# Dilation-4 score products with stationary operands from tiles ordered by residue of 4, and value tiles of 65 columns

## The chip, the cores and the metric

One core of a Trainium2 chip runs the whole program. The metric is the device time of one execution, in microseconds (us); the lower the better. The kernel before was timed three times: 3049.63, 3056.54 and 3057.88 us, median 3056.54 us.

## The reference

One layer of an encoder over 2048 positions in float32: RMSNorm, a combined projection, eight heads of dilated attention, four mLSTM heads, an output projection, a convolutional GLU feed-forward block, a gated per-layer embedding, and a final norm. The change touches the attention alone. Of it this much matters:

```
ATTN_HEADS = 8; ATTN_HEAD_DIM = 64; SEQ = 2048
ATTN_PATTERNS = ((128, 1), (512, 4), (2048, 16))      # (window, dilation)

def dilated_branch(q, k, v, dil, n_side):
    M = S // dil
    def to_res(t):                                     # residue classes of the positions
        return t.reshape(B, H, M, dil, hd).transpose(0, 1, 3, 2, 4)
    o, lse = banded_attention(to_res(q), to_res(k), to_res(v), n_side)
    ...

def dilated_mixture_attention(q, k, v, positions):
    ...
    for window, dil in ATTN_PATTERNS:
        o, l = dilated_branch(q, k, v, dil, (window // 2) // dil)
        outs.append(o); lses.append(l)
    wts = jax.nn.softmax(jnp.stack(lses, axis=0), axis=0)
    out = jnp.sum(wts[..., None] * jnp.stack(outs, axis=0), axis=0)
```

Each head sees every query against 64 keys on either side in three patterns: neighbours (dilation 1), every fourth position (dilation 4) and every sixteenth (dilation 16). The three are joined by their softmax denominators, so one set of exponentials against one row maximum per query, summed over the three patterns, gives the same result.

## The kernel before

All of it is in the class Attention (L823 to L1137). A head's scores are computed in 16 units of 128 rows for each pattern, called p = 0 (dilation 1), p = 1 (dilation 4) and p = 2 (dilation 16). They are computed twice.

**pass_a** gets the row maxima. Its stationary operand is queries (128 of them), its moving operand a window of keys; each unit takes two matmuls (L949 and L950, a main part and a low part of 65 rows), DVE adds a mask and takes the maximum (L958). It goes in 20 steps: p = 0 in 8 steps of two units, p = 1 in 8 of two, p = 2 in 4 of four. Then come transposes (L962) and a small exchange through DRAM that leaves the negated maxima in a row of qm2.

**pass_b** makes the output, with keys stationary and queries moving (L991, L992 in `weights`). ACT takes the exponential (L996), POOL clears what lies outside the band (L930, L932), and three steps later (LOOK = 3) `values` multiplies by the value tile vt, whose last 64 columns are ones, so that the same product gives the denominators (L1017 for p = 2, L1037 for the others). ACT copies the p = 2 result to oacc (L1018), DVE adds the others (L1047). The steps are p = 2 first (4 steps), then p = 1 (8 steps, called s1 to s8 here), then p = 0 (8 steps).

**The two passes overlap.** `run` takes one step of the stream (pass_a of the next head, and what hangs on it) beside each step of pass_b: step n of pass_b of head h stands beside step 9 + n of pass_a of head h + 1, and after twelve steps beside the first steps of head h + 2. In steady state one head takes one period. At a period's start stand `outputs` of the head just finished: denominators from DRAM and back (zc, zr_d, zb), and two products of 64x1024 on DVE that make att (L1080).

**Layouts.** qs, ks1 and ks2 are loaded in the order of positions (L863 to L865). For dilation 16, km1, km2, qm1 and qm2 hold them ordered by residue of 16. They are made by casts whose source has a stride of 64 bytes: ACT makes km1 (L875), DVE makes km2 and qm1 (L877), four pieces of 512 columns each. For dilation 4 there is no such tile: `unit` returns as stationary operand a slice of qs, ks1 or ks2 with a stride of four elements,

```
t0 = r + 512 * j
return (lambda t: t[:, t0:t0 + 509:4]), ...
```

**Pages.** The large tiles (qs, ks1, ks2, km1, km2, qm1, qm2, vt, oacc, att) take pages from one pool of 22 of 2080 floats per partition. A tile that is asked for when none is free waits until an older one has had its last reader. The pairs of e and the tiles zb share another pool of four. Every engine works through its own queue in order; the order in each queue is set when the kernel is built, by a scheduler that sees dependences and free pages.

Of the kernel before, what the change touches and what calls it, by code (L numbers as in the profile page):

```python
# [828 lines left out]
class Attention:  # L829


    def __init__(self, g, pool, psA):
# [10 lines left out]

        def load_v(h, p):
            if h == 0:
                vt.append(page(g, [P, 16, P], F32, name="vt"))
                nc.gpsimd.memset(vt[p][:, :, HD:], 1.0)
            src, dst = g.vd[h], vt[p][:, :, :HD]
            if p == 0:
                nc.sync.dma_start(dst, src.rearrange("(j p) c -> p j c", p=P))  # L850
            elif p == 1:
                for r in range(4):
                    nc.sync.dma_start(dst[:, 4 * r:4 * r + 4], src.rearrange("(j p r) c -> r p j c", p=P, r=4)[r])
            else:
                nc.sync.dma_start(dst, src.rearrange("(p r) c -> p r c", r=16))

        def load(h):
            H = Head()
            H.qs = page(g, [P, S], F32R, name="qs")
            H.ks1 = page(g, [P, S], F32R, name="ks1")  # L860
            H.ks2 = page(g, [65, S], F32R, name="ks2")
            for s in range(2):
                nc.sync.dma_start(H.qs[64 * s:64 * s + 64].bitcast(F32), g.qk[0, s, h])  # L863
                nc.sync.dma_start(H.ks1[64 * s:64 * s + 64].bitcast(F32), g.qk[1, 0, h])
            nc.sync.dma_start(H.ks2.bitcast(F32), g.kl[h])  # L865
            return H
# [12 lines left out]
        def keys_by_residue(H, q):  # L879
# [4 lines left out]
            to_residues(nc.scalar, H.km1, H.ks1, q)  # L884
            to_residues(nc.vector, H.km2[:64], H.ks2[:64], q)

        def queries_by_residue(H, q):
            if q == 0:
                H.qm1 = page(g, [P, S], F32R, name="qm1")
                H.qm2 = page(g, [65, S], F32R, name="qm2")  # L890
            to_residues(nc.vector, H.qm1, H.qs, q)
            if q == 3:
                nc.sync.dma_start(H.qm2[:64].bitcast(F32), H.qm1[:64].bitcast(F32))

        def unit(p, i):


            if p == 0:
                lo, hi = max(0, 8 * i - 4), min(P, 8 * i + 12)
                return (lambda t: t[:, P * i:P * i + P]), (lambda t: residues(t)[:, :, lo:hi]), lo, hi, lo - (8 * i - 4)  # L900
            if p == 1:
                r, j = divmod(i, 4)
                lo, hi = max(0, 32 * j - 16), min(P, 32 * j + 48)
                t0 = r + 512 * j
                return (lambda t: t[:, t0:t0 + 509:4]), (lambda t: t.rearrange("p (b r a) -> p r b a", r=4, a=P)[:, r, :, lo:hi]), lo, hi, lo - (32 * j - 16)
            return (lambda t: t[:, P * i:P * i + P]), (lambda t: t[:, P * i:P * i + P]), 0, P, 0

        def width(p, lo, hi):
# [28 lines left out]
        def pass_a(h, H):  # L937

            mst = pool.tile([P, 3, 16], F32, name="mst", tag="mst", bufs=2)
            for p in (0, 1, 2):  # L940
                per = 4 if p == 2 else 2
                W = 512 // per
                for i0 in range(0, 16, per):
                    ps = psA.tile([P, 512], F32, name="psa", tag="psa")
                    for u in range(per):
                        st, win, lo, hi, off = unit(p, i0 + u)
                        o = shape3(p, ps[:, u * W:u * W + width(p, lo, hi)], lo, hi)
                        q = st(H.qm1 if p == 2 else H.qs)
                        nc.tensor.matmul(o, lhsT=q, rhs=win(H.km1), start=True, stop=False)  # L949
                        nc.tensor.matmul(o, lhsT=q[:65], rhs=win(H.km2), start=False, stop=True)  # L950
                    for u in range(per):
# [26 lines left out]
        def weights(h, H, p, i0):  # L978
# [9 lines left out]
            for u in range(per):  # L988
                st, win, lo, hi, off = us[u]
                o = shape3(p, ps[:, u * W:u * W + widths[u]], lo, hi)  # L990
                nc.tensor.matmul(o, lhsT=st(H.km1 if p == 2 else H.ks1), rhs=win(H.qm1), start=True, stop=False)  # L991
                nc.tensor.matmul(o, lhsT=st(H.km2 if p == 2 else H.ks2), rhs=win(H.qm2), start=False, stop=True)  # L992
            for u0, u1 in ([(0, per)] if min(widths) == W else [(u, u + 1) for u in range(per)]):
                cs = slice(u0 * W, (u1 - 1) * W + widths[u0])
                st, win, lo, hi, off = us[u0]
# [13 lines left out]
        def values(h, H, p, i0, ew):  # L1009
# [2 lines left out]
            W = 128 if p == 2 else 256  # L1012
            if p == 2:
                b = i0 // 4
                o = self.psO.tile([P, 512], F32, name="pso", tag="pso")
                for u in range(4):
                    nc.tensor.matmul(o[:, P * u:P * u + P], lhsT=vt[2][:, i0 + u, :], rhs=e[:, P * u:P * u + P], start=True, stop=True)  # L1017
                nc.scalar.activation(oacc[:, 512 * b:512 * b + 512], o, AF.Copy)  # L1018
# [3 lines left out]
            for u in range(2):  # L1022
# [7 lines left out]
                for b, x0, x1 in pieces:  # L1030
                    first = b not in banks
                    if first:
                        banks[b] = self.psO.tile([P, 512], F32, name="pso", tag="pso")
                    base = 0 if p == 1 else 32 * b
                    o = banks[b].rearrange("p (x y) -> p x y", y=A)[:, :, x0 - base:x1 - base]
                    m = shape3(p, e[:, cs], lo, hi)[:, :, x0 - lo:x1 - lo]
# [10 lines left out]
                    nc.vector.tensor_tensor(o, o, banks.pop(b).rearrange("p (x y) -> p x y", y=A), ALU.add)  # L1047

        def pass_b(h, H):
            H.oacc = page(g, [P, S], F32, name="oacc")  # L1050
            H.banks = {}
            steps = [(2, i) for i in range(0, 16, 4)] + [(p, i) for p in (1, 0) for i in range(0, 16, 2)]
            pend = []
            for k, (p, i0) in enumerate(steps):
                pend.append((p, i0, weights(h, H, p, i0)))
                if p == 2 and i0 == 12:
                    H.km1 = H.km2 = None
                if len(pend) > LOOK:
                    values(h, H, *pend.pop(0))
                yield  # L1060
# [25 lines left out]
        def stream():  # L1086
            for q in range(4):
                keys_by_residue(heads[0], q)
            for h in range(AH):
                H = heads[h]  # L1090
                n = 0
                for _ in pass_a(h, H):
                    n += 1
                    if n == 10 and h + 1 < AH:
                        heads[h + 1] = load(h + 1)
                    if n in (7, 9, 11, 13):
                        queries_by_residue(H, (n - 7) // 2)
                    if n in (14, 16, 18, 20) and h + 1 < AH:
                        keys_by_residue(heads[h + 1], (n - 14) // 2)
                    yield  # L1100
                H.qs = None

        def start():
            heads[0] = load(0)
# [1242 lines left out]
```

## Time and profile before

| what | value |
|---|---|
| time, median of three | 3056.54 us |
| the profiled execution's time | 3060.42 us |
| its span | 3058.6 us |
| PE busy in the span | 94% |
| DVE, ACT, POOL busy | 66%, 42%, 35% |
| mean granted clock of PE | 0.958 |
| one head's period in the attention | 49.5 us |

The span is one execution from its first instruction to its last; 1.8 us lie around it. The attention's steady state runs from about 720 us to some 1010 us of the span. PE is the engine of matmuls and PEld its loading of stationary operands, which overlaps it; a granted clock of 1.0 is 2.4 GHz and 0.5 is 1.2 GHz. Each load of a stationary operand belongs to one matmul; the distance between the starts of two loads in a row is what one product takes on PE when nothing else holds it.

### The profile page before, as it was taken

The numbers are of one execution on the slowest core, as the hardware profiler recorded it, in microseconds if no ns is written. First come the engines' busy times: TensorE is split into PE (matmuls) and PEld (weight loads), VectorE is DVE, ScalarE is ACT, GpSimd is POOL, SyncE is SP. The second block draws the span as 40 slices with busy tenths as digits, with TensorE's granted clock in tenths as the row PEclk, the third lists the DMA queues.
The fourth block names the chain that finished last, engine by engine and source line by source line (L and its number), as shares of the span: only waits on it lengthen the run. The fifth ranks groups of instructions, "written<-read, shape, count | busy, mean of one in ns | idle before, by whom it ended". The sixth has DMA issues, their size and how long they took to land.

```text
span 3058.6 us, 41026 instructions
## 1 busy us (share of the span) xinstructions
PE 2875.3 (94%) x14474; PEld 2437.7 (80%) x14474; DVE 2032.9 (66%) x4107; ACT 1278.4 (42%) x2428; POOL 1084.5 (35%) x1146
## 2 busy tenths in 40 slices
PE   8889899889999898898899998899999999999999
PEld 7867888789999787786688886688887777877887
DVE  5856796666665488335877777977776566746444
ACT  5555465424333356223544444444444322224332
POOL 2133423416555454001433333433334230433221
PEclk9999999879999999999899999899999999999999
DMA  7744425475554374565222223222225876765111
GB/s 213 213 138 131 140 84 178 130 150 120 121 118 108 107 252 132 141 201 186 69 83 83 79 75 119 66 78 80 83 83 167 315 251 216 245 222 182 44 44 44
DMA packets 386798, 419.77 MB, mean 137 GB/s; under 512 B 107457, under 2 KB 300865, under 8 KB 380945
## 3 DMA queue, kind: packets, MB, share of 16 engines
q1 hardware_dynamic: 386592, 417.16, 44.9%
q8 instruction: 114, 1.87, 0.3%
q14 instruction: 92, 0.75, 0.1%
HBM read 308.16 MB, written 104.61 MB: 135 GB/s over the span
## 4 chain that ended last, share of the span: by engine, by line
PE 46%; DVE 7%; DMA 5%; issue 3%; POOL 3%; ACT 1%; SPq 1%; POOLq 0%; DVEq 0%; ACTq 0%
PE ps L1811 8%; PE ps L1812 8%; PE ps L1813 8%; PE ps L149 6%; PE ps L147 6%; PE ps L148 6%; DMA ar<-a_d 2%; POOL ar L175 1%; DVE fw L176 1%; DVE as L176 1%; DMA wdr<-in_w_ffn_down_dram 1%; PE psm L1480 1%; PE psm L1481 1%; PE psm L1389 1%; DVE bl L176 1%
## 5 line engine op out<-in xcount | busy, mean ns | idle before, releaser
L1811 PE MATMUL ps<-bh,fw 128*128 128x512 f32 x1232 | 495.7, 403 | 28.9 <-ACT fw L176 11.4
L1813 PE MATMUL ps<-bh,fw 128*128 128x512 f32 x1232 | 491.3, 399 | 6.8 <-DVE fw L176 6.7
L1812 PE MATMUL ps<-bl,fw 128*128 128x512 f32 x1232 | 492.9, 400 | 4.1 <-DVE bl L176 3.2
L175 POOL TENSOR_TENSOR sum<-fraw 128x512 f32<-128x512 f32 x132 | 197.7, 1498 | 406.6 <-DVE fw L176 360.2
L1811 PEld LDWEIGHTS ps<-bh,fw 128*128 128x128 f32 x1232 | 236.1, 192 | 94.0 <-ACT fw L176 13.7
L1813 PEld LDWEIGHTS ps<-bh,fw 128*128 128x128 f32 x1232 | 236.2, 192 | 64.6 <-DVE fw L176 10.0
L1812 PEld LDWEIGHTS ps<-bl,fw 128*128 128x128 f32 x1232 | 236.1, 192 | 60.9 <-DVE bl L176 7.4
L147 PE MATMUL ps<-wd,as 128*128 128x512 f32 x616 | 246.1, 399 | 13.8 <-ACT as L176 13.8
L149 PE MATMUL ps<-wd,as 128*128 128x512 f32 x616 | 246.1, 400 | 6.6 <-DVE as L176 6.5
L175 POOL TENSOR_TENSOR ar<-ar 128x768 f32<-128x768 f32 x80 | 141.1, 1785 | 298.7 <-DMA ar<-a_d 220.3
L148 PE MATMUL ps<-wd,as 128*128 128x512 f32 x616 | 244.7, 397 | 0.0
L176 ACT ACTIVATE fw<-sum 128x512 fp32r<-128x512 f32 x220 | 134.6, 628 | 241.7 <-DVE sum L175 142.7
L176 DVE TENSOR_TENSOR fw<-sum,fw 128x512 fp32r<-128x512 f32 x220 | 214.2, 988 | 7.9 <-ACT fw L176 7.7
L176 ACT ACTIVATE as<-ar 128x768 fp32r<-128x768 f32 x108 | 85.0, 792 | 273.6 <-POOL ar L175 222.6
L996 ACT ACTIVATE e<-psb 128x512 f32<-128x512 f32 (+2 forms) x240 | 95.7, 437 | 218.4 <-PE psb L992 205.8
L176 DVE TENSOR_TENSOR as<-ar,as 128x768 fp32r<-128x768 f32 x108 | 111.1, 1037 | 110.1 <-ACT as L176 109.9
L930 POOL TENSOR_SCALAR_AFFINE_SELECT e<-e 128x64 f32<-128x64 f32 (+2 forms) x225 | 102.3, 455 | 202.0 <-ACT e L996 197.6
L1884 POOL TENSOR_TENSOR act<-act,up 128x512 f32<-128x512 f32 x88 | 129.4, 1470 | 87.8 <-DVE up L1833 68.8
L958 DVE CUSTOM_DVE_ANT_0 junk<-psa,mask 128x256 bf16<-128x256 f32 (+1 forms) x304 | 111.7, 367 | 71.9 <-PE psa L950 62.4
L147 PEld LDWEIGHTS ps<-wd,as 128*128 128x128 f32 x616 | 117.4, 191 | 42.9 <-ACT as L176 16.9
L149 PEld LDWEIGHTS ps<-wd,as 128*128 128x128 f32 x616 | 117.3, 190 | 38.8 <-DVE as L176 12.1
L1875 DVE SCALAR_TENSOR_TENSOR act<-ext,fcw,act 128x512 f32<-128x512 f32 (+1 forms) x176 | 136.4, 815 | 16.7 <-ACT act L1873 16.0
(359 smaller groups left out, 7735.9 us busy)
## 6 DMA issues: line engine op xcount, KB each, us to landing
ar<-a_d SPq DMA_DIRECT2D x94, 384.0 KB
ar<-a_d SPq DMA_DIRECT2D x94, 320.0 KB
wdr<-in_w_ffn_down_dram SPq DMA_DIRECT2D x50, 512.0 KB
fraw<-in_w_ffn_gate_dram SPq DMA_DIRECT2D x22, 1024.0 KB
fraw<-in_w_ffn_up_dram SPq DMA_DIRECT2D x22, 1024.0 KB
a_d<-act SPq DMA_DIRECT2D x88, 256.0 KB
xT_d<-xT SPq DMA_DIRECT2D x32, 512.0 KB
bx<-xT_d SPq DMA_DIRECT2D x16, 1024.0 KB
```

Of the source, the lines that this page charges most:

```text
L147: g.nc.tensor.matmul(out, lhsT=sh, rhs=mh, start=start, stop=False)
L148: g.nc.tensor.matmul(out, lhsT=sh, rhs=ml, start=False, stop=False)
L149: g.nc.tensor.matmul(out, lhsT=sl, rhs=mh, start=False, stop=stop)
L175: eng[0].tensor_tensor(src, a, b, ALU.add if sign > 0 else ALU.subtract)
L176: return (lambda: g.nc.scalar.activation(hi, src, AF.Copy)), (lambda: eng[1].tensor_tensor(lo, src, hi.bitcast(F32), ALU.subtract))
L930: nc.gpsimd.affine_select(l, l, pat + [[s, half - off]], ALU.is_ge, 0.0, base=s * off + w, channel_multiplier=-1)
L958: nc.vector.tensor_tensor_reduce(shape3(p, junk[:, :n], lo, hi), o, m, 1.0, -3e38, ALU.add, ALU.max, mst[:, p, i:i + 1])
L1811: nc.tensor.matmul(ps, lhsT=w[:, 0, k], rhs=h[:, k], start=start and k == 0, stop=False, skip_group_check=True)
L1812: nc.tensor.matmul(ps, lhsT=w[:, 0, k], rhs=l[:, k], start=False, stop=False, skip_group_check=True)
L1813: nc.tensor.matmul(ps, lhsT=w[:, 1, k], rhs=h[:, k], start=False, stop=k == 3, skip_group_check=True)
L1875: nc.vector.scalar_tensor_tensor(act, ext[a][:, lo + k:hi + k], self.cw[:, k, f:f + 1], act, ALU.mult, ALU.add)
L1884: nc.gpsimd.tensor_tensor(act, act, up[a][:, lo:hi], ALU.mult)
```

## The change

New tiles hold the queries and keys ordered by residue of 4: q4, k41 and k42. Each is made from qs, ks1 or ks2 by four ACT copies of 512 columns (`to_four`), whose source has a stride of 16 bytes and whose destination is contiguous: twelve copies a head, 96 in all. The p = 1 products of both passes take contiguous slices of them as stationary operand; the moving operands stay as they are. The copies of q4 stand at steps 2, 4, 6 and 8 of the stream, those of k41 and k42 at steps 17 to 20. qs is released at step 13 rather than at the pass's end.

The value tile shrinks from 128 to 65 columns (one column of ones), its three tiles take two pages rather than three, and oacc and its PSUM tiles have 65 partitions in use.

```
-                vt.append(page(g, [P, 16, P], F32, name="vt"))
-                nc.gpsimd.memset(vt[p][:, :, HD:], 1.0)
+                if p != 1:
+                    vt.append(page(g, [P, 2 - p // 2, 16, HD + 1], F32, name="vt"))
+                    nc.gpsimd.memset(vt[p][:, :, :, HD:], 1.0)
+                    vt[p:] = [vt[p][:, i] for i in range(2 - p // 2)]
...
+        def by_four(t):
+            return t.rearrange("p (r m) -> p r m", r=4)
+
+        def to_four(dst, src, r):
+            nc.scalar.activation(by_four(dst)[:, r], src.bitcast(F32).rearrange("p (m r) -> p r m", r=4)[:, r], AF.Copy)
+
+        def queries_by_four(H, r):
+            if r == 0:
+                H.q4 = page(g, [P, S], F32R, name="q4")
+            to_four(H.q4, H.qs, r)
+
+        def keys_by_four(H, r):
+            if r == 0:
+                H.k41 = page(g, [P, S], F32R, name="k41")
+                H.k42 = page(g, [65, S], F32R, name="k42")
+            to_four(H.k41, H.ks1, r)
+            to_four(H.k42, H.ks2, r)
...
-                t0 = r + 512 * j
-                return (lambda t: t[:, t0:t0 + 509:4]), ...
+                return (lambda t: t[:, P * i:P * i + P]), ...
...
-                        q = st(H.qm1 if p == 2 else H.qs)
+                        q = st((H.qs, H.q4, H.qm1)[p])
...
-                nc.tensor.matmul(o, lhsT=st(H.km1 if p == 2 else H.ks1), rhs=win(H.qm1), start=True, stop=False)
-                nc.tensor.matmul(o, lhsT=st(H.km2 if p == 2 else H.ks2), rhs=win(H.qm2), start=False, stop=True)
+                nc.tensor.matmul(o, lhsT=st((H.ks1, H.k41, H.km1)[p]), rhs=win(H.qm1), start=True, stop=False)
+                nc.tensor.matmul(o, lhsT=st((H.ks2, H.k42, H.km2)[p]), rhs=win(H.qm2), start=False, stop=True)
...
-                o = self.psO.tile([P, 512], F32, name="pso", tag="pso")
+                o = self.psO.tile([P, 512], F32, name="pso", tag="pso")[:HD + 1]
...
-            H.oacc = page(g, [P, S], F32, name="oacc")
+            H.oacc = page(g, [HD + 1, S], F32, name="oacc")
...
+                if p == 1 and i0 == 14:
+                    H.k41 = H.k42 = None
...
+                    if n in (2, 4, 6, 8):
+                        queries_by_four(H, (n - 2) // 2)
                     if n in (7, 9, 11, 13):
                         queries_by_residue(H, (n - 7) // 2)
+                    if n == 13:
+                        H.qs = None
+                    if n == 16:
+                        H.q4 = None
+                    if 17 <= n < 21:
+                        keys_by_four(H, n - 17)
                     if n in (14, 16, 18, 20) and h + 1 < AH:
                         keys_by_residue(heads[h + 1], (n - 14) // 2)
                     yield
-                H.qs = None
```

Since the queues are ordered by a scheduler, the new copies and the changed demand for pages move other instructions. Three places of one period in the middle of the attention show it.

ACT, from step s3 of p = 1 on, before. Each p = 1 step has one exponential 192 wide and one 256 wide.

```order
L996 ACTIVATE e<-psb 128x192
L996 ACTIVATE e<-psb 128x256
L1018 ACTIVATE oacc<-pso 128x512
L996 ACTIVATE e<-psb 128x256
L996 ACTIVATE e<-psb 128x192 x2
L996 ACTIVATE e<-psb 128x256 x2
L996 ACTIVATE e<-psb 128x192 x2
L996 ACTIVATE e<-psb 128x256 x2
L996 ACTIVATE e<-psb 128x192 x2
L996 ACTIVATE e<-psb 128x256
```

The same stretch after; L895 is the copy of `to_four`, with k for k41 (9247) and k42 (9248) and q for q4.

```order
L895 ACTIVATE k_9247<-ks_8453 128x512
L1017 ACTIVATE e<-psb 128x256
L1017 ACTIVATE e<-psb 128x192
L895 ACTIVATE k_9247<-ks_8453 128x512 x3
L1017 ACTIVATE e<-psb 128x192
L1017 ACTIVATE e<-psb 128x256 x2
L1017 ACTIVATE e<-psb 128x192 x2
L1017 ACTIVATE e<-psb 128x256
L895 ACTIVATE k_9248<-ks_8454 65x512 x4
L895 ACTIVATE q_9435<-qs 128x512
L1017 ACTIVATE e<-psb 128x256
L1017 ACTIVATE e<-psb 128x192
```

The twelve copies stand between exponentials that followed each other before: one after s3, three after s4, five after s7, three more after s8.

DVE, around the two products att of `outputs`, before. mask1 is the mask of p = 1, mask2 that of p = 2.

```order
L958 ISA junk_7330,mst_7033<-psa_7323,mask1_5786 128x256
L958 ISA mst_7033 128x1
L877 CAST km2_7362<-ks2_7249 64x512
L1080 TENSOR_TENSOR att_7392<-oacc_6663,zb_7279 64x8x128
L877 CAST km2_7362<-ks2_7249 64x512
L958 ISA junk_7357,mst_7033<-psa_7352,mask1_5786 128x256
L958 ISA mst_7033 128x1
L1080 TENSOR_TENSOR att_7392<-oacc_6663,zb_7281 64x8x128
```

And after, where the maxima of p = 2 are already in front of it.

```order
L979 ISA junk_7520,mst_7061<-psa_7509,mask2_5794 128x128
L979 ISA mst_7061 128x1
L979 ISA junk_7522,mst_7061<-psa_7509,mask2_5794 128x128
L979 ISA mst_7061 128x1
L1103 TENSOR_TENSOR att_7425<-oacc_6681,zb_7312 64x8x128
L979 ISA junk_7524,mst_7061<-psa_7509,mask2_5794 128x128
L979 ISA mst_7061 128x1
L1103 TENSOR_TENSOR att_7425<-oacc_6681,zb_7314 64x8x128
```

The first att stood behind one or two of the four casts of km2 and the early p = 1 maxima; now all four casts, the last three p = 1 maxima among them, and seven maxima of p = 2 stand between the landing of ks2 and the first att.

SP, the queue that issues the loads, before: the loads of qs and ks1 of the head after next stand in the middle of the period, between those of vt.

```order
L855 DMA vt_6589<-vd_d_59 128x16x64
L863 DMA qs_7818<-qk_d_57 64x2048
L853 DMA vt_6583<-vd_d_59 128x4x64
L864 DMA ks1_7819<-qk_d_57 64x2048
L863 DMA qs_7818<-qk_d_57 64x2048
L853 DMA vt_6583<-vd_d_59 128x4x64
L864 DMA ks1_7819<-qk_d_57 64x2048
```

And after, at the boundary of two periods.

```order
L866 DMA qs_7866<-qk_d_57 64x2048
L867 DMA ks1_7867<-qk_d_57 64x2048
L852 DMA vt_6597<-vd_d_59 128x16x64
L1091 DMA zc_7841<-oacc_7257 128x1x16
L866 DMA qs_7866<-qk_d_57 64x2048
L867 DMA ks1_7867<-qk_d_57 64x2048
L868 DMA ks2_7868<-kl_d_58 65x2048
L1094 DMA zr_d_65<-zc_7841 128x16
```

The loads of qs, ks1 and ks2 have moved to the end of one period and the start of the next, where vt and zc are loaded too.

## Rows read from the trace of the kernel before

**Rows 1.** Periods: PE, PEld, DVE, ACT, POOL busy (xcount), clock, DMA share, GB/s.

```profile
819.23:868.71 49.48, 49.48 (x304) 48.49 (x304) 31.57 (x119) 18.05 (x38) 27.82 (x61) 0.93 0.54 119
```

**Rows 2.** Waits in the period 819.23 to 868.71: engine, line, releaser: us, times, longest.

```profile
ACT e L996 <- PE psb L992: 29.8, 18, 5.5
```

**Rows 3.** Timeline of PEld, p=2 and p=1: start, duration, instruction.

```profile
839.94 0.19 PEld L949 LDWEIGHTS psa<-km,qm 128*128 128x128 f32 x1
840.05 0.19 PEld L950 LDWEIGHTS psa<-km,qm 65*128 65x128 f32 x1
...
841.07 0.33 PEld L991 LDWEIGHTS psb<-qm,ks 128*128 128x128 f32 x1
841.30 0.33 PEld L992 LDWEIGHTS psb<-qm,ks 65*128 65x128 f32 x1
```

**Rows 4.** Timeline of PEld, the same products in p=0.

```profile
850.55 0.19 PEld L992 LDWEIGHTS psb<-qm,ks 65*128 65x128 f32 x1
850.66 0.19 PEld L991 LDWEIGHTS psb<-qm,ks 128*128 128x128 f32 x1
```

**Rows 5.** Timeline of PEld in a stretch at half clock.

```profile
776.19 0.33 PEld L991 LDWEIGHTS psb<-qm,km 128*128 128x128 f32 x1
776.40 0.33 PEld L992 LDWEIGHTS psb<-qm,km 65*128 65x128 f32 x1
```

**Rows 6.** Windows inside the period, same columns as rows 1.

```profile
826.00:832.50 6.50, 6.50 (x31) 6.50 (x31) 3.67 (x5) 4.70 (x8) 2.81 (x4) 0.55 0.76 165
...
850.40:868.70 18.30, 18.30 (x126) 17.70 (x125) 11.44 (x45) 4.80 (x10) 10.87 (x23) 1.00 0.30 69
```

**Rows 7.** ACT groups by form, 720-950 us: xcount | busy, mean ns | idle.

```profile
L875 ACT ACTIVATE km<-ks 128x512 fp32r<-128x512 f32 x20 | 20.9, 1097 | 0.0
```

**Rows 8.** The page's costliest groups: an ACT copy with a contiguous source.

```profile
L176 ACT ACTIVATE fw<-sum 128x512 fp32r<-128x512 f32 x220 | 134.6, 628 | 241.7 <-DVE sum L175 142.7
```

**Rows 9.** Timeline of ACT, a late p=1 step and the first of p=0.

```profile
844.45 0.60 ACT L996 ACTIVATE e<-psb 128x256 f32<-128x256 f32 x2 [1.97 <-PE psb L992]
...
851.29 0.60 ACT L996 ACTIVATE e<-psb 128x192 f32<-128x192 f32 x2 [1.05 <-PE psb L992]
```

**Rows 10.** Timeline of POOL, last selection of the first p=0 step.

```profile
852.74 0.40 POOL L932 TENSOR_SCALAR_AFFINE_SELECT e<-e 128x128 f32<-128x128 f32 x1
```

**Rows 11.** Timeline of PE, value products of the first p=0 step.

```profile
856.18 0.92 PE L1037 MATMUL pso<-e,vt 128*128 128x192 f32 x4
856.76 0.47 PE L949 MATMUL psa<-km,qs 128*128 128x256 f32 x1
```

**Rows 12.** Groups on DVE by form, 719 to 950 us.

```profile
L958 DVE CUSTOM_DVE_ANT_0 junk<-psa,mask 128x256 bf16<-128x256 f32 x96 | 40.6, 423 | 26.6 <-PE psa L950 24.4
...
L958 DVE CUSTOM_DVE_ANT_0 junk<-psa,mask 128x128 bf16<-128x128 f32 x80 | 23.3, 291 | 13.1 <-PE psa L950 10.4
...
L958 DVE DVE_READ_ACCUMULATOR2_ANT mst<- 128x1 f32 x224 | 18.6, 83 | 0.0
...
L877 DVE CAST km<-ks 64x512 fp32r<-64x512 f32 x20 | 12.9, 650 | 0.0
```

**Rows 13.** Timeline of DVE at a period's start.

```profile
823.67 0.25 DVE L1070 RECIPROCAL zc<-zc 128x16 f32<-128x16 f32 x1 [1.44 <-DMA zc<-oacc]
...
829.26 1.94 DVE L1080 TENSOR_TENSOR att<-oacc,zb 64x1024 f32<-64x1024 f32 x1 [2.83 <-DMA zb<-zr_d]
...
831.32 2.02 DVE L1080 TENSOR_TENSOR att<-oacc,zb 64x1024 f32<-64x1024 f32 x1
```

**Rows 14.** Timeline of SP, loads at the boundary.

```profile
814.34 0.33 SPq L865 DMA_DIRECT2D ks<-kl_d  x1
...
820.35 1.15 SPq L1068 DMA_DIRECT2D zc<-oacc  x1
```

**Rows 15.** DMA view of 780 to 870 us, 40 slices: GB/s moved.

```profile
GB/s 153 0 233 4 227 243 62 240 216 217 95 0 124 11 0 47 189 0 226 15 46 253 178 0 175 58 217 249 117 269 181 230 36 23 105 4 0 33 204 0
```

**Rows 16.** Timeline of ACT ahead of the first pass_b.

```profile
678.00 1.28 ACT L996 ACT_TABLE_LOAD   x1 [30.50 <-PE psb L992]
```

More of the change, by code (lines that the diff above doesn't have):

```diff
@@ L858, in load @@
             H = Head()
+            H.q4 = H.qm1 = H.k41 = H.k42 = None
             H.qs = page(g, [P, S], F32R, name="qs")
@@ L903, in unit @@
                 lo, hi = max(0, 32 * j - 16), min(P, 32 * j + 48)
-                t0 = r + 512 * j
-                return (lambda t: t[:, t0:t0 + 509:4]), (lambda t: t.rearrange("p (b r a) -> p r b a", r=4, a=P)[:, r, :, lo:hi]), lo, hi, lo - (32 * j - 16)
+                return (lambda t: t[:, P * i:P * i + P]), (lambda t: t.rearrange("p (b r a) -> p r b a", r=4, a=P)[:, r, :, lo:hi]), lo, hi, lo - (32 * j - 16)
             return (lambda t: t[:, P * i:P * i + P]), (lambda t: t[:, P * i:P * i + P]), 0, P, 0
@@ L1032, in values @@
                     if first:
-                        banks[b] = self.psO.tile([P, 512], F32, name="pso", tag="pso")
+                        banks[b] = self.psO.tile([P, 512], F32, name="pso", tag="pso")[:HD + 1]
                     base = 0 if p == 1 else 32 * b
```

## The prediction

> **What bounds the kernel now.** The change lives in the attention, so I first cut its steady state into periods of one head. A period takes 49.5 us; in it PE shows 49.5 us busy, DVE 31.6, POOL 27.8 and ACT 18.1 [rows 1]. The reader should see one full engine and three with room. The waits say the same: ACT waits 29.8 us of a period for score products of PE [rows 2]. So PE bounds the period, and what shortens a PE product there shortens the kernel, until another engine is late.
>
> Then the loads of the stationary operand, one by one. The distance between two starts is what a product takes. From contiguous tiles it is 0.11 us (839.94 to 840.05); with a stride of four elements it is 0.23 (841.07 to 841.30) [rows 3]. That this is the stride and not the moving operand is shown by the same lines in p = 0, where the slice is contiguous: 0.11 again [rows 4]. At half clock a contiguous product takes 0.21 [rows 5], so there the gain is almost gone.
>
> **Part by part: PE.** A group of one p = 1 step has two units of two products. Strided it takes 4 x 0.235 = 0.94 us; contiguous 4 x 0.113 = 0.45, or up to 0.58 where the 256 columns of the moving operand set the pace; I take 0.51, a gain of 0.43. A period has 8 such groups of pass_a and 8 of pass_b: 16 x 0.43 = 6.9 us. Over 8 heads that is 55 us, if PE stays what bounds it.
>
> The value tile of 65 columns shortens a load; it helps only where the load and not the moving operand sets the pace, in the 12 products of a period with 64 columns. They can't go under half of 0.11, so at most 12 x 0.055 = 0.66 us a period; I take 0.6. The copies to oacc keep 512 columns on 65 partitions: nothing. A period in which PE stays busy would take 49.5 - 6.9 - 0.6 = 42.0.
>
> **The copies on ACT.** Twelve a period, 512 columns each, source stride 16 bytes. No row shows this form. The nearest from above is the cast to km1, the same shape with a stride of 64 bytes: 1.10 us, 1.04 when several follow one another [rows 7]. The nearest from below is a copy of 512 contiguous columns, 0.63 [rows 8]. I take 1.04: PE's reads at the stride of 16 bytes cost twice the contiguous ones [rows 3], and 1.04 is nearly twice 0.63 too. That is 12.5 us of ACT a period. Together with its 18.1 it has 30.6 of work: enough room as a sum, so what matters is where the copies stand.
>
> The order answers that. Eleven of the twelve come after step s3, three to five at a time, in front of exponentials that PE's value products need. Before, ACT was idle for about 2 us ahead of each such exponential [rows 9], so 8 steps give some 13 us of cover for 12.5 us of copies, if the copies could start early. They can't: k41 takes the page of the old oacc, which is read until the second att.
>
> **When att is done.** T counts from a period's start (819.23 before). Before, the two att products started at T = 10.0 and 12.1, when the denominators were there [rows 13]. Now DVE comes to them only after four casts of km2, and these wait for ks2, whose load has moved to the boundary. Before, ks2 was issued 5 us ahead of it [rows 14]. Now SP issues it behind the load of zc, at T = 1.1 before [rows 14], and two more loads. Busy slices of the DMA view move 204 to 269 GB/s [rows 15], so 0.52 MB takes about 2.2 us; four such transfers (vt, a half of qs, a half of ks1, ks2) from T = 0.4 end at 9.2. A small transfer takes 2 us from issue to use (zc, 820.35 to 823.67 with its issue of 1.15 [rows 13, 14]), so the casts start near 11.0. Behind them on DVE, in the new order: 4 x 0.65 for the casts, 3 x 0.5 for maxima of p = 1, 7 x 0.37 for maxima of p = 2 [rows 12]: 11.0 + 2.6 + 1.5 + 2.6 = 17.7. First att 17.7 to 19.7, a maximum 0.4, second att to 22.0 (1.94 and 2.02 each [rows 13]); since the maxima run in part while ks2 is on its way I take 0.4 off: 19.3 and 21.6.
>
> **ACT from there.** The exponentials of s3 take the buffer of the first zb, free at 19.3; the first copy of k41 takes the page free at 21.6. From there ACT never waits: one copy 1.1 (22.7), s4 0.6, three copies 3.1 (26.4), s5 to s7 1.8 (28.2), five copies 5.2 (33.4), s8 0.6, three copies 3.1 (37.1), the first step of p = 0 0.6: 37.7. Before, that exponential ended at 851.89, T = 32.7 [rows 9]. Its selection on POOL ended 1.25 us behind it (852.74 + 0.40 [rows 10]) and its value products take 0.58 (856.18 to 856.76 [rows 11]): 39.5. Before they ended at T = 37.5, because PE and not ACT set the pace. What follows them took 868.71 - 856.76 = 12.0 us; with one shorter p = 1 group (0.43) and the 64-column products (0.6) 11.0. The period is 50.5, 1.0 longer than before.
>
> The clock comes on top. Before, one stretch of each period ran at half clock (0.55 granted from 826.0 to 832.5) and the p = 0 stretch at 1.00 [rows 6]. Now PE waits between T = 10 and 37, so more of it will be at half clock; while PE waits that costs nothing. It costs only in the last 11 us, where some 45 products would take 0.10 more each: between 0 and 4.5. I take 0.9, near the lower end, since before the clock was whole in that stretch [rows 6]. A period of 51.4: +1.9.
>
> **The sum.** Eight heads have six full periods with both outputs and copies: 6 x 1.9 = +11.4. The first pass_b has no outputs ahead of it, so no att holds it: of its 3.4 us of own gain (8 groups) I take 2. The last one has no stream beside it: 8 groups, -3. The copies ahead of the first pass_b lie in 30.5 us in which ACT is idle [rows 16]; its pass_a is set by DVE: 0 to -1, I take -0.5. In all +5.9 on the profiled 3060.4; the median of the runs shown is 3.9 lower, so 3056.5 + 5.9 = **3062**. About 0.3% (9 us, 3047 to 3066) is what a measurement of this kernel can tell from no change; this is within it. The gain of 50 us on PE goes into an ACT queue that is late.
>
> **A rule against the row.** PE's reads show the price of a 16-byte stride: 0.23 for 0.11 [rows 3]. The Trainium skill, SBUF — State Buffer, section Specifications (TRN2), says that SBUF has lines of 16 bytes, that two hits a line are needed for full bandwidth, and that each crossing pays. By that rule a stride of four float32 elements pays on every element, for ACT as for PE, and the copies cost what the 64-byte cast costs; the trace agrees for PE, and no run here shows it for ACT. If ACT did not pay, the first rival's sum would hold.
>
> **Rivals.** *The copies are cheap.* At 0.63 a copy, the twelve save 12 x 0.41 = 4.9 us of that chain: -3.0 a period for +1.9; 6 x -3.0 - 5.5 = -23.5, so 3033. For it: the lower bound is a measured row. Against: PE's reads at this stride.
>
> *PE stays the bound.* If the dependences on att come free earlier than I place them, the 2 us of idle time ahead of each exponential hide all copies: 42 a period, 6 x -7.5 - 5.5 = -50, so 3006. For it: the sums of busy time. Against: DVE's order and the page that k41 waits for.
>
> *Slower: the clock stays down.* If PE's waiting up to T = 37 leaves the p = 0 stretch at half clock, it costs 4.5 instead of 0.9 a period: 6 x 3.6 = 22, so 3084. It decides from about 1.6 us a period on. For it: half clock already costs one stretch of each period [rows 6]. Against: the stretch behind it was at 1.00.
>
> *Slower: the loads come late.* If the six loads at the boundary share the DMA engines with vt's and land 2 us later, DVE's casts, att and the whole ACT chain are 2 us later: 6 x 2 = 12, so 3074.
>
> *It doesn't do what it says.* If the contiguous copies were read no faster, ACT would still have idle time and nothing would change: 3056 to 3064. Rows 4 speak against it.
>
> **How the numbers follow.** My forecast has 0.45: 0.33 of that within 0.3%, 0.10 above and 0.02 below. Cheap copies 0.16 (faster), PE the bound 0.10 (faster), the clock 0.15 and late loads 0.10 (slower), no effect 0.04 (same). Faster 0.28, within 0.3% 0.37, slower 0.35. The range leaves out PE as the bound, and the ends of the cheap copies and of the clock: 3032 to 3085, some 0.8.
>
> **What would show it.** Right: periods of 50 to 52 us with PE well under full; L992's successor in p = 1 at 0.11 to 0.12 a product; copies of about 1.04 us; ACT without idle time between T = 22 and 37; att at T = 17 to 22. Wrong: copies of 0.6 us, a period near 42 with PE full, att before T = 14, or a p = 0 stretch at a clock of 0.5.

## The result

The changed kernel is slower: 3079.42 us, median of four runs (3078.25 to 3083.59), beside 3055.56 for the kernel before. The ratio is 1.0088, interval 1.0066 to 1.0110: +24 us. The forecast was 3062 us with a range of 3032 to 3085; the time lies in the range, on the side of the rivals that are slower. A few executions, one each of e7_split_behind, e8_vt65 and e11_q4_zb among them, took 3498 to 4713 us at a lower clock; the medians below include them, the ratios do not.

First the busy time, from the page of the changed kernel.

```profile
PE 2840.4 (92%) x14474; PEld 2373.9 (77%) x14474; DVE 2035.3 (66%) x4107; ACT 1369.5 (44%) x2524; POOL 1084.9 (35%) x1145
```

PE has 35 us less of busy time, ACT 91 more. Two windows of one period each, columns as in [rows 1]:

```profile
776.86:831.46 54.60, 44.90 (x305) 39.84 (x304) 31.61 (x121) 29.30 (x50) 27.86 (x61) 0.87 0.54 109
831.46:886.70 55.24, 45.64 (x306) 41.00 (x304) 31.13 (x121) 29.40 (x50) 28.31 (x61) 0.85 0.53 107
```

A period that took 49.5 us [rows 1] takes 54.1 to 55.2. PE is busy for 45 of them, where it was busy throughout. Five such periods and the two at the ends make the attention end 30 us later in the profiled run (last value product at 1090.6 us of the span, 1060.9 before); what lies behind it is the same code, and took 7 us less in this execution; why is not shown.

The PE loads of one p = 1 group, as in [rows 3] and [rows 4]:

```profile
783.15 0.19 PEld L1012 LDWEIGHTS psb<-qm,k 128*128 128x128 f32 x1
783.28 0.19 PEld L1013 LDWEIGHTS psb<-qm,k 65*128 65x128 f32 x1
783.39 0.19 PEld L1012 LDWEIGHTS psb<-qm,k 128*128 128x128 f32 x1
783.50 0.19 PEld L1013 LDWEIGHTS psb<-qm,k 65*128 65x128 f32 x1
```

They stand 0.11 to 0.13 apart, where the strided ones stood 0.23 apart. So the products became as cheap as forecast, and the time went elsewhere. The copies, as groups on ACT (mean ns of one behind the count):

```profile
L895 ACT ACTIVATE q<-qs 128x512 fp32r<-128x512 f32 x16 | 17.7, 1195 | 0.0
...
L895 ACT ACTIVATE k<-ks 128x512 fp32r<-128x512 f32 x16 | 17.2, 1129 | 3.1 <-DVE att L1103 3.1
```

Now one period in order of time. T counts from its start at 776.86. The loads on SP, and the trip of the denominators among them (zc, zr_d, zb):

```profile
772.76 0.47 SPq L866 DMA_DIRECT2D qs<-qk_d  x1
...
777.97 2.54 SPq L1091 DMA_DIRECT2D zc<-oacc  x1
...
781.83 0.56 SPq L868 DMA_DIRECT2D ks<-kl_d  x1
784.94 0.35 SPq L1094 DMA_DIRECT2D zr_d<-zc  x1
...
794.06 1.09 SPq L1098 DMA_DIRECT2D zb<-zr_d  x2
```

ks2 (the load at 781.83) and zr_d are issued early; zb can only be issued at 794.06, T = 17.2, nine us after zr_d. DVE in the same stretch:

```profile
784.66 0.25 DVE L1093 RECIPROCAL zc<-zc 128x16 f32<-128x16 f32 x1 [3.90 <-DMA zc<-oacc]
...
793.66 0.58 DVE L880 CAST km<-ks 64x512 fp32r<-64x512 f32 x1 [5.55 <-DMA ks<-kl_d]
...
799.51 1.90 DVE L1103 TENSOR_TENSOR att<-oacc,zb 64x1024 f32<-64x1024 f32 x1
...
801.47 1.93 DVE L1103 TENSOR_TENSOR att<-oacc,zb 64x1024 f32<-64x1024 f32 x1
```

The first cast of km2 waits 5.55 us for ks2, which lands at T = 16.8; the first att starts at T = 22.7. Before, it started at T = 10.0 [rows 13]. Then ACT:

```profile
789.94 3.91 ACT L878 ACTIVATE km<-ks 128x512 fp32r<-128x512 f32 x4 [4.53 <-DMA ks<-qk_d]
...
801.49 0.61 ACT L1017 ACTIVATE e<-psb 128x192 f32<-128x192 f32 x2 [1.65 <-DVE att L1103]
...
803.43 1.14 ACT L895 ACTIVATE k<-ks 128x512 fp32r<-128x512 f32 x1 [0.85 <-DVE att L1103]
...
815.08 3.28 ACT L895 ACTIVATE q<-qs 128x512 fp32r<-128x512 f32 x3
818.14 2.16 ACT L1017 ACTIVATE e<-psb 128x192 f32<-128x192 f32 x5
821.88 0.60 ACT L1017 ACTIVATE e<-psb 128x512 f32<-128x512 f32 x1 [1.58 <-POOL e L951]
```

ACT waits for ks1 until T = 13.1, with exponentials of p = 2 queued behind the four casts; the exponential of s3 waits for att until T = 24.6, and the first copy of k41 for the second att until T = 26.6. From there to 820.3 it has no idle time. PE, meanwhile, waits 5.7 us for a maximum that stands behind the first of the waiting casts on DVE:

```profile
794.64 0.47 PE L970 MATMUL psa<-km,qm 128*128 128x128 f32 x1 [5.70 <-DVE mst L979]
```

### The profile page after: what moved, and what is told of

Read it like the earlier page. It is cut to its first block, busy times and chain, and to the rows that moved or that the text cites. A ratio compares the mean times of both kernels' runs of the same rounds, so it can differ in the third digit from the quotient of the medians.

```text
span 3081.7 us, 41178 instructions
## 1 busy us (share of the span) xinstructions
PE 2840.4 (92%) x14474; PEld 2373.9 (77%) x14474; DVE 2035.3 (66%) x4107; ACT 1369.5 (44%) x2524; POOL 1084.9 (35%) x1145
## 4 chain that ended last, share of the span: by engine, by line
PE 41%; DVE 8%; DMA 7%; POOL 4%; issue 3%; ACT 2%; SPq 0%; POOLq 0%; DVEq 0%; ACTq 0%
PE ps L1841 8%; PE ps L1843 7%; PE ps L1842 7%; PE ps L149 5%; PE ps L147 5%; PE ps L148 5%; DMA ar<-a_d 3%; POOL ar L175 2%; DVE as L176 1%; DVE fw L176 1%; DMA wdr<-in_w_ffn_down_dram 1%; DVE wd L176 1%; DVE act L1905 1%; DVE bl L176 1%; PE psm L1510 1%
## 5 line engine op out<-in xcount | busy, mean ns | idle before, releaser
L1843 PEld LDWEIGHTS ps<-bh,fw 128*128 128x128 f32 x1232 | 236.1, 192 | 64.4 <-DVE fw L176 10.1
```

The source lines that it names most:

```text
L1843: nc.tensor.matmul(ps, lhsT=w[:, 1, k], rhs=h[:, k], start=False, stop=k == 3, skip_group_check=True)
```

## The experiments

Each ratio is to the kernel before, as timed beside that run (medians 3052.71 to 3056.25 us).

**Cheap copies.** What are the copies' durations worth, with everything else in its place?

```
-  nc.scalar.activation(by_four(dst)[:, r], src.bitcast(F32).rearrange("p (m r) -> p r m", r=4)[:, r], AF.Copy)
+  nc.scalar.activation(by_four(dst)[:, r], by_four(src.bitcast(F32))[:, r], AF.Copy)
```

> The changed kernel with a contiguous source in the twelve copies (each quarter is copied as it lies, so the columns are the wrong ones and the values too). The order and the pages are those of the changed kernel; only a copy's time falls, from 1.04 to about 0.6. If ACT's queue from the second att on sets the period's end, each period gets 12 x 0.43 = 5 us shorter: 3079 - 6 x 5 = about 3048. If the late loads alone set it, or PE's clock, at most 1 us a period: above 3070.

Measured: 3051.62 us, ratio to the kernel before 0.9988 (0.9977 to 0.9999). That is 28 us less than the changed kernel, 31 were expected. One copy and one period:

```profile
L895 ACT ACTIVATE q<-qs 128x512 fp32r<-128x512 f32 x20 | 11.4, 621 | 0.0
```

```profile
763.00:813.80 50.80, 43.93 (x305) 39.95 (x303) 31.21 (x120) 23.53 (x50) 25.69 (x61) 0.87 0.58 116
```

ACT's queue behind att sets the end of a period, and most of a copy's price goes into it: ACT is busy for 23.5 us of a period rather than 29.3, which is 5.8 less, and the period is 54.6 - 50.8 = 3.8 shorter.

**The casts out of the way.** Theory L: the loads that moved to the boundary stand, through the casts that need them, in front of exponentials and of att. Theory A, its rival, puts the loss down to the ACT time of the copies.

```
-  if n in (14, 16, 18, 20) and h + 1 < AH:
-      keys_by_residue(heads[h + 1], (n - 14) // 2)
+  if 17 <= n < 21 and h + 1 < AH:
+      keys_by_residue(heads[h + 1], n - 17)
```

> The changed kernel with the casts to km1 and km2 called at steps 17 to 20 of the stream rather than 14, 16, 18 and 20. The loads stay at the boundary; but the casts that wait for them no longer stand in front of the exponentials of p = 2 on ACT and of att on DVE. Theory L: att starts at T = 12 to 15 rather than 22.7, and the period falls by 4 to 6 us, time 3045 to 3055. Theory A: the copies take the same time on ACT, the period stays within 1 us, time 3073 to 3080.

Measured: 3079.56 us, ratio 1.0083 (1.0063 to 1.0104): no change against the changed kernel. By its numbers theory L falls. But the trace says why: the casts no longer hold att, and att waits all the same, for zb. It starts at T = 20.4 (period from 831.2), only 2.3 us earlier. The DVE line, the two DMAs on SP, and the casts to km1 on ACT:

```profile
851.64 1.88 DVE L1103 TENSOR_TENSOR att<-oacc,zb 64x1024 f32<-64x1024 f32 x1 [6.64 <-DMA zb<-zr_d]
```

```profile
837.43 0.35 SPq L1094 DMA_DIRECT2D zr_d<-zc  x1
...
848.16 1.09 SPq L1098 DMA_DIRECT2D zb<-zr_d  x2
```

```profile
862.66 4.00 ACT L878 ACTIVATE km<-ks 128x512 fp32r<-128x512 f32 x4
```

zr_d is issued at 837.43 and zb, which needs it, at 848.16: the transfer of 8 KB takes 10.7 us, behind the loads of qs, ks1 and ks2. In the kernel before, where those loads stood elsewhere, it was 1.55 us:

```profile
823.95 0.34 SPq L1071 DMA_DIRECT2D zr_d<-zc  x1
...
825.50 1.10 SPq L1075 DMA_DIRECT2D zb<-zr_d  x2
```

So the loads delay att twice, once through the casts and once through the trip of the denominators, and taking one away leaves the other. What att gained was spent again: the four casts to km1, 4.0 us of ACT, now stand behind att in the queue that sets the period's end. That the trip is late because it is issued behind the loads is theory D, which the next run tests.

**The loads behind the denominators.** As above, and

```
-  if n == 10 and h + 1 < AH:
+  if n == 14 and h + 1 < AH:
       heads[h + 1] = load(h + 1)
```

> As e4_keys_late, and the loads of qs, ks1 and ks2 are called at step 14 of the stream rather than 10, so that on SP they stand behind zc, zr_d and zb of the head just finished. Theory D (it is the trip of the denominators, zc, zr_d and zb, that stands behind 3 MB of loads in the DMA queues; in e4_keys_late zb landed at T = 20.4, before at 10.0): zb lands at T = 9 to 11, att is done at T = 14, and with the 28 us that the changed kernel takes from the second att to the period's end the period is 43 to 47 us, time 3030 to 3045. If the trip is late for another reason, or PE's clock takes what is won, the period stays above 52, time above 3068.

Measured: 3066.58 us, ratio 1.0034 (1.0022 to 1.0046): 13 us won, 34 or more expected. att is early now, and the next wait is the one that was moved:

```profile
838.68 3.85 DVE L1103 TENSOR_TENSOR att<-oacc,zb 64x1024 f32<-64x1024 f32 x2
...
848.85 1.61 DVE L880 CAST km<-ks 64x512 fp32r<-64x512 f32 x3 [4.09 <-DMA ks<-kl_d]
```

```profile
852.84 0.38 PE L983 MATMUL psa<-ident,mst 128*16 128x128 f32 x1 [8.75 <-DVE mst L979]
```

att starts at T = 16.4 (period from 822.3) and no longer waits for zb. The casts of km2 now wait 4.1 us for ks2, with the last maxima queued behind them, and PE's transposes wait 8.75 us for those. Theory D is right in its mechanism and the size of its gain was wrong: the loads, now issued at T = 8.3 to 12.5, come late for the casts instead, and km1's casts still stand behind att on ACT.

**Eight of the twelve copies on DVE.** As above, and for q4 and k42

```
-  to_four(H.q4, H.qs, r) ... to_four(H.k42, H.ks2, r)
+  to_four_v(H.q4, H.qs, r) ... to_four_v(H.k42, H.ks2, r)   # nc.vector.tensor_copy
```

> As e6_loads_behind, with the copies to q4 and k42 on DVE rather than ACT (eight of a head's twelve; the casts of DVE at a stride of 64 bytes took 0.64 to 0.65 us, those of ACT 1.04 to 1.10). ACT gets 8.3 us a period less, DVE 5.2 more. If ACT's queue still sets the period in e6_loads_behind, another 2 to 4 us a period go: 3015 to 3030. If what remains is the trip of the denominators and PE's clock, it is within 5 us of e6_loads_behind.

Measured: 3067.89 us, ratio 1.0035 (1.0019 to 1.0050): as e6_loads_behind. ACT, with 21.5 us of work a period, no longer sets its end; PE's transposes wait 9.1 us in the period from 823.0 for maxima behind the same casts. The copies themselves, as a group on DVE:

```profile
L895 DVE CAST k<-ks 65x512 fp32r<-65x512 f32 x16 | 10.2, 640 | 0.0
```

**No copies at all.** How much is PE's part worth, with nothing to pay for it? The kernel leaves out the reordering: q4, k41 and k42 are not made, and p = 1 takes contiguous slices of the unordered tiles.

```
-  q = st((H.qs, H.q4, H.qm1)[p])
+  q = st(H.qm1 if p == 2 else H.qs)
-  lhsT=st((H.ks1, H.k41, H.km1)[p]) ... lhsT=st((H.ks2, H.k42, H.km2)[p])
+  lhsT=st(H.km1 if p == 2 else H.ks1) ... lhsT=st(H.km2 if p == 2 else H.ks2)
-  queries_by_four(H, (n - 2) // 2) ... keys_by_four(H, n - 17)
...
```

> The changed kernel without q4, k41 and k42: no copies and no new pages; the p = 1 stationary operands are contiguous slices of qs, ks1 and ks2 as they lie, so their columns are the wrong ones (the values are not the reference's, the work of every other engine is). It prices the PE gain alone, with the 65-column value tile. Theory L (the loss comes from loads of qs, ks1 and ks2 that move to the period's boundary because the new tiles take their pages) and theory A (the loss comes from the ACT time of the copies) both expect the period to fall from 49.5 to about 42 us and the time to about 3006. If PE's gain is not real, the time stays near 3056.

Measured: 3043.97 us over ten runs from 3031.69 to 3057.56, ratio 0.9962 (0.9944 to 0.9980). 50 us were expected and 12 came: both theories missed. Two periods of the one profiled run:

```profile
763.90:809.20 45.30, 41.04 (x304) 37.40 (x303) 31.14 (x121) 17.85 (x38) 28.56 (x61) 0.96 0.65 130
714.20:763.90 49.70, 47.79 (x306) 42.65 (x305) 31.75 (x121) 17.32 (x38) 29.39 (x61) 0.83 0.57 119
```

The first took 45.3 us at a mean clock of 0.96, the second 49.7 at 0.83, with the same work. And in the first PE waits, which it did not do before:

```profile
776.25 0.60 ACT L1017 ACTIVATE e<-psb 128x192 f32<-128x192 f32 x2 [2.67 <-DVE att L1101]
```

```profile
778.44 1.94 PE L1038 MATMUL pso<-e,vt 128*65 128x128 f32 x8 [3.93 <-ACT oacc L1039]
```

It waits for the copy of p = 2 to oacc, which on ACT stands behind an exponential that waits for att. So in that period 3.9 of the 7.5 us go into the wait for the denominators, which PE's slower products used to cover. In the second period PE waits for 1.8 us in all, and is at half clock for some 17. The ten executions show the clock as well: the fastest, 3031.69 us, has a mean clock of 0.96, the slowest, 3057.56, one of 0.951.

**The copies without pages.** As e1_no_copies, and

```
-  to_four(H.q4, H.qs, r) ... to_four(H.k41, H.ks1, r) ... to_four(H.k42, H.ks2, r)
+  to_scratch(H.qs, r) ... to_scratch(H.ks1, r) ... to_scratch(H.ks2, r)   # one [P, 512] tile
```

> As e1_no_copies, but the twelve ACT copies of a head are made, at the same steps, into one scratch tile that nobody reads; they take ACT's time and no page. Theory L: the loads stay early as before, ACT has idle time to hide most of 12.5 us, period 42 to 45, time 3010 to 3025. Theory A: the copies stand in front of exponentials as in the changed kernel and the period stays above 49, time 3050 to 3080.

Measured: 3088.32 us, ratio 1.0103 (1.0067 to 1.0138): above what either theory gave. It can't tell the theories apart as meant: without a page to wait for, the copies stand where their source is late. In the period from 841.0, four copies of qs wait for its load, with the exponential of s8 behind them:

```profile
872.53 4.55 ACT L900 ACTIVATE scratch<-qs 128x512 fp32r<-128x512 f32 x4 [5.19 <-DMA qs<-qk_d]
```

What it does show is that freed pages alone don't hide the copies.

**q4 alone.** The changed kernel with

```
-  lhsT=st((H.ks1, H.k41, H.km1)[p]) ... lhsT=st((H.ks2, H.k42, H.km2)[p])
+  lhsT=st(H.km1 if p == 2 else H.ks1) ... lhsT=st(H.km2 if p == 2 else H.ks2)   # stride of 4 for p = 1
-  if 17 <= n < 21:
-      keys_by_four(H, n - 17)
```

> The changed kernel with q4 alone: pass_a's p = 1 products take contiguous slices of q4, pass_b's stay strided (no k41, no k42). Four copies a head rather than twelve, and one page more than before, which the smaller value tile gives back: the loads stay in the middle of the period. PE gains 8 x 0.43 + 0.6 = 4.0 us a period, ACT gets 4.2. Theory D: zb as early as before, period 46 to 48, time 3035 to 3048. Theory A: four copies are a third of the loss of twelve, 3056 to 3065.

Measured: 3073.33 us, ratio 1.0042 (1.0029 to 1.0055): above what either theory gave. Two periods:

```profile
821.10:875.60 54.50, 51.69 (x305) 46.58 (x304) 31.67 (x120) 21.79 (x42) 27.71 (x61) 0.78 0.48 108
932.60:980.15 47.55, 44.40 (x305) 41.05 (x304) 31.50 (x121) 21.90 (x42) 27.59 (x61) 0.96 0.31 69
```

The second, at a mean clock of 0.96, takes 47.6 us; the first, at 0.78, takes 54.5, with the same matmuls. What differs is the clock: 3.4 us at half clock in the second, 23.9 in the first (T = 13.7 to 37.6). PE waits about the same in both, 2.8 us in the first and 3.2 in the second, mostly shortly before or as the clock falls. The first also moves more bytes (108 GB/s for 69); a run below has that the other way round.

**PE's wait taken away, as meant.** zb in a page of its own, so that the exponentials no longer wait for att to return a buffer. Once without copies, once with q4.

```
-  zb.append(raw(g, [64, 1024], name="zb"))
+  zp = page(g, [64, 2, 1024], F32, name="zb")
...
```

> As e1_no_copies (contiguous slices of the unordered tiles, so values are not the reference's; no copies), with the two halves of zb in a page of their own rather than in two of the four buffers that the exponentials share. In e1_no_copies PE waited 3.9 us a period because the exponential of s1 or s3 waited for att to give back its buffer, and the clock fell there. Theory E (that wait, and the clock that falls with it, is where PE's 7.5 us a period went): PE never waits, the period is 42 to 43.5 us, time 3008 to 3020. If the rest of the gain was lost elsewhere, it stays at 45 and the time at 3032 to 3058 as in e1_no_copies.

> As e5_q4 (q4 alone, four copies on ACT, pass_b's operands strided), with zb in a page of its own. Theory E: PE's wait of 2.4 us a period goes, the half clock behind it (24 us a period in e5_q4) falls to at most the 6.8 us of the kernel before, period 45.5 to 46.5, time 3033 to 3042. If the four copies are what costs, it stays near 3073.

Measured: e10_zb_page_nc 3058.38 us, ratio 1.0002 (0.9985 to 1.0019); e11_q4_zb 3082.10 us, ratio 1.0084 (1.0065 to 1.0103). In e10_zb_page_nc, two periods, and a stretch of a third one:

```profile
821.50:874.80 53.30, 50.25 (x306) 44.85 (x303) 31.37 (x121) 17.61 (x38) 30.34 (x61) 0.78 0.55 110
929.90:973.95 44.05, 41.32 (x305) 37.35 (x303) 31.02 (x121) 17.60 (x38) 30.25 (x61) 0.96 0.33 74
```

```profile
783.90:804.30 20.40, 20.14 (x80) 17.48 (x81) 12.15 (x55) 3.02 (x10) 10.18 (x27) 0.50 0.88 162
```

PE's wait is shorter than in e1_no_copies and not gone: 3.1 us in the first period (1.1 for ACT's copy to oacc, 1.9 for a maximum on DVE), 2.7 in the second. In the stretch PE is busy for 20.1 of 20.4 us, and the clock stands at 0.50 through it. The period of 44.05 us has 3.4 us of half clock and the one of 53.30 has 23.9: 9.3 us for 20.5, or 0.45 us for each. So theory E falls as it was put: a shorter wait brought no shorter stretch at half clock. Both times are above what theory E gave, and e11_q4_zb above its other branch too. e11_q4_zb, with waits of 4 us, is at the low clock for 20 us or more in five periods of six:

```profile
772.80:828.10 55.30, 51.34 (x305) 46.16 (x304) 33.03 (x121) 21.80 (x42) 26.71 (x61) 0.78 0.48 107
```

**The old value tile.** The kernel before with only the p = 1 operand contiguous.

```
-  t0 = r + 512 * j
-  return (lambda t: t[:, t0:t0 + 509:4]), ...
+  return (lambda t: t[:, P * i:P * i + P]), ...
```

> The kernel before with nothing changed but the p = 1 stationary operand, which is a contiguous slice of the unordered qs, ks1 and ks2 (the values are not the reference's): value tiles of 128 columns, no copies, pages and loads as before. Beside e1_no_copies it tells whether the value tile has a share in the long stretches at half clock. Theory V (it has): at most 6.8 us a period at half clock, period 44 to 45, time 3020 to 3028. Theory E2 (any kernel whose PE waits in the first 15 us of a period risks the long stretch, whatever the value tile): as e1_no_copies, 3032 to 3058.

Measured: 3045.43 us, ratio 0.9971 (0.9954 to 0.9987), as e1_no_copies. Theory V falls; the old value tile has a long stretch at half clock too. Its two extreme periods:

```profile
719.10:763.65 44.55, 41.22 (x306) 38.67 (x304) 31.91 (x119) 17.32 (x38) 28.74 (x61) 1.00 0.62 133
902.70:957.40 54.70, 51.22 (x306) 49.10 (x304) 31.17 (x119) 17.89 (x38) 28.50 (x61) 0.78 0.27 60
```

44.55 us at full clock throughout, 54.70 with 23.9 us at half: 10.1 for 23.9, 0.42 us for each. In the first PE's waits are short (1.4 us at most), in the second there is one of 3.5. Here the slow period is the one with less DMA traffic, 60 GB/s for 133, so more traffic is not what brings the long stretch.

**The value tile alone**, operands strided as before, and the same with zb in a page of its own (the edit of e10_zb_page_nc):

```
-  vt.append(page(g, [P, 16, P], F32, name="vt"))
+  if p != 1:
+      vt.append(page(g, [P, 2 - p // 2, 16, HD + 1], F32, name="vt"))
...
-  H.oacc = page(g, [P, S], F32, name="oacc")
+  H.oacc = page(g, [HD + 1, S], F32, name="oacc")
```

> The kernel before with the value tile of 65 columns and oacc of 65 partitions alone; stationary operands strided as before, no copies. PE gains 0.3 to 0.66 us a period: 3051 to 3055. If the page that it frees moves loads, up to 10 us either way.

> As e8_vt65 (the kernel before with the 65-column value tile; all operands strided), with zb in a page of its own. PE never waits in e8_vt65, so the buffer of zb can win nothing there: 3046 to 3054 if the page of zb is harmless. If zb's own page is what made e10 and e11 slower than e1 and e5 (by 14 and 9 us), it is slower than e8_vt65 by 8 us or more, 3059 or above.

Measured: e8_vt65 3051.31 us, ratio 0.9975 (0.9962 to 0.9989); e9_zb_page 3042.46 us, ratio 0.9954 (0.9936 to 0.9972). A period of each:

```profile
768.30:817.00 48.70, 48.70 (x305) 45.70 (x303) 31.64 (x120) 18.00 (x38) 27.54 (x61) 0.93 0.59 121
```

```profile
765.10:813.70 48.60, 48.60 (x304) 45.61 (x303) 31.64 (x121) 18.00 (x38) 27.54 (x61) 0.93 0.60 121
```

The value tile gives the 0.6 to 0.8 us a period that its loads were costed at. The page for zb is harmless here, where PE never waits; that it is harmless with contiguous operands too is not shown. What can be said of e10_zb_page_nc is that its executions are as fast as those of e1_no_copies at the same mean clock (at 0.953: 3042.3 and 3052.19 beside 3052.96) and are more often at a lower one. e9_zb_page lies below its expected range; beside the kernel before, as timed with each, it is 6 to 7 us better than e8_vt65, the intervals overlap, and their periods are alike, so a gain from the page is not shown. It is the fastest kernel of this study that computes the whole layer as before, 12 us under the kernel before and 37 under the changed one.

## Why the prediction was right in part

**Right.** PE's price: 0.11 to 0.13 a product. The price of a copy: 1.04 was taken, of bounds from 0.63 to 1.10; the means of the groups are 1.13 to 1.20, and in a row each takes 1.05 to 1.1. Where the gain goes: into ACT's queue, late behind att. From the second att to the end of the period the working gave 51.4 - 21.6 = 29.8 us; it took 54.6 - 26.6 = 28.0. The rival of the cheap copies was priced right too: e3_cheap is 28 us under the changed kernel, and the working put that rival 29 us under the forecast. On copies with a 16-byte stride the Trainium skill, SBUF — State Buffer, section Specifications (TRN2), is borne out for ACT: 1.13 to 1.20 us against 0.62 contiguous. DVE's copies at the same stride took 0.61 to 0.64, and no run here has DVE make them from a contiguous source.

**The step that failed** is the landing of ks2, in the part on when att is done: T = 11.0 in the working, 16.8 in the trace. It was put together from four transfers of 2.2 us from T = 0.4 on. The windows show what came:

```profile
774.00:782.00 8.00, 8.00 (x67) 7.40 (x66) 4.38 (x18) 1.20 (x2) 2.34 (x7) 1.00 1.05 205
782.00:790.00 8.00, 5.94 (x45) 5.21 (x44) 2.91 (x15) 1.25 (x3) 1.80 (x1) 0.90 1.06 197
```

The DMA engines are full from 774 to 790, at 200 GB/s rather than 240: 2.6 us a transfer. The first halves of qs and ks1, counted as gone, were issued at T = -4.1 and still in flight; and the copy of qm2, issued at T = 8.5, shares the engines. From 774.0 to 793.7 some 3.7 MB pass. The rival of the late loads had the right mechanism, with 2 us for what was 5.8. With it the second att ends 5.0 us later than in the working, and what follows is 1.8 shorter: 6 x 3.2 = 19 on the forecast, 3081 for the 3079 measured.

That the time still lies in the range is partly luck: by the rival of the late loads it would have been 3074, and the range reached 3085 because of the rival of the clock (3084), which did not come about. By the prediction's own signs the period (54.1 to 55.2 us for 50 to 52) and the first att (T = 22.7 for 17 to 22) came out later than was forecast.

That the same loads also delay zr_d and zb stood nowhere in the working. It had DVE's order as the only thing in front of att, and e4_keys_late shows a second one close behind it: without the first, att starts at T = 20.4 rather than 22.7.

**The clock** was forecast to cost 0.9 us a period, in the last stretch. In the changed kernel it cost nothing there:

```profile
776.86:788.40 11.54, 10.54 (x89) 9.99 (x87) 5.21 (x26) 2.38 (x4) 3.39 (x5) 1.00 1.06 200
788.40:802.20 13.80, 8.10 (x40) 7.91 (x40) 8.22 (x28) 7.27 (x14) 5.06 (x13) 0.51 0.49 92
802.20:831.46 29.26, 26.26 (x182) 21.93 (x181) 18.17 (x68) 19.65 (x33) 19.42 (x44) 1.00 0.36 81
```

It falls at T = 11.6, at the start of PE's wait of 5.7 us and after 1 us of shorter ones, and is back at full by 25.3; the last 29 us are at 1.00. The rival in which the clock decides that stretch did not come about here.

**What both sides of the working took for granted** is that the gain on PE is there to be had: 42 us a period where PE stays the bound, 3006 in all. The runs without copies show that it isn't. Even at full clock throughout, the period of e12_nc_vt128 is 44.6 us, with PE busy for 41.2 of it. And the products that were strided have become sensitive to the clock: a strided product takes 0.23 to 0.24 us at either clock, a contiguous one 0.11 or 0.21 [rows 3, 5]. The strided ones at half clock, in the kernel before, from the stretch of [rows 5]:

```profile
775.09 0.33 PEld L950 LDWEIGHTS psa<-km,qs 65*128 65x128 f32 x1
775.32 0.33 PEld L949 LDWEIGHTS psa<-km,qs 128*128 128x128 f32 x1
```

At half clock almost all of the gain is gone, and these kernels spend up to 24 us of a period there.

What stays open is why the clock stays at half for 3.4 us in one period and for 23.9 in another with the same matmuls. The length of PE's wait ahead of it does not tell: 3.9 us went before a short stretch in e1_no_copies, 3.5 before a long one in e12_nc_vt128, and 2.4 to 3.1 before either in e5_q4 and e10_zb_page_nc. Nor is it the value tile or the DMA traffic (e12_nc_vt128). In the kernel before it falls in each period for 6.8 us [rows 6], while PE is busy.

## What to carry to other kernels

A layout copy is priced with three things beside its own duration: the page it takes, the loads that move because that page is no longer free, and whatever small transfer is then issued behind those loads. Before a bound engine is made faster, look at what its slow pace covers: here it covered a wait for the denominators' trip through DRAM (3.9 us in a period of e1_no_copies) and a clock to which the strided products are indifferent. When removing one wait changes nothing, look in the trace for a second one that ends at nearly the same time.

## What the runs showed of the hardware

- A read at a stride of 16 bytes costs ACT as much as one at 64: 1.13 to 1.20 us for 512 columns (means, changed kernel) beside 1.05 to 1.10, and 0.62 contiguous (e3_cheap). DVE takes 0.61 to 0.64 for the same copy in e7_split_behind, about what its casts at 64 bytes take there (0.60 to 0.61).
- A stationary operand read at a stride of 16 bytes makes a product take 0.23 to 0.24 us at either clock; a contiguous one takes 0.11 at full clock and 0.21 at half.
- zr_d, a DMA of 8 KB, issued behind loads of 0.5 MB took 8 to 11 us from its issue until zb, which needs it, could be issued (changed kernel and e4_keys_late); in e6_loads_behind, with the loads behind it, and in the kernel before, 1.5 to 3.
- Periods of the same matmuls took 44.05 us with 3.4 us at half clock and 53.3 with 23.9 in one execution (e10_zb_page_nc), with PE waiting for 2.7 and 3.1 us.
- In the kernel before the clock fell to half for 6.8 us of a period in which PE had no idle time.
